# Second attention: a pair's scores in single PSUM banks, read by two VectorE instructions per head

## The chip, the cores and the metric

The kernel runs on one core of one Trainium2 chip. The metric is the device time of one execution in microseconds, the median over several runs. Times in stages and of single instructions come from one profiled execution. PE is TensorE's matmul, PEld its weight load, DVE VectorE, ACT ScalarE, POOL GpSimd, SP the engine whose queue issues the DMAs.

## The reference

A trunk of two layers over 1024 latent tokens and 256 context tokens of width 1024, in float32. Layer 0 mixes tokens by neighbourhood attention (16 heads of 64), layer 1 by sliding-window attention, and each ends with a gated feed-forward part with a short convolution. The change is in layer 1's attention: 16 query heads in 4 groups, each group with one key head and one value head. A block of 128 queries sees its own 128 keys, the 128 before and the 128 after, cut to a distance of 128, and all 256 context keys; a logit per head (the sink) enters the softmax without a value.

```python
def sliding_window_attention(q, k, v, k_c, v_c, sink):
    band = np.abs(qoff[:, None] - koff[None, :]) <= SWA_RADIUS
    ctx_ok = jnp.ones((Q_BLOCK, n_ctx), bool)
    def block_step(j):
        ...
        valid = band & ((kpos >= 0) & (kpos < seq))[None, :]
        mask = jnp.concatenate([valid, ctx_ok], axis=-1)
        return attend(q_j, jnp.concatenate([k_j, k_c], axis=1), jnp.concatenate([v_j, v_c], axis=1),
                      mask=mask, sink=sink)
```

`attend` scales the products by 1/8, adds the mask, takes the softmax over keys and sink in float32 and multiplies by the values.

## The kernel before

The program is one long recording of operations on five engines. Each big stage (first attention, its feed-forward part, second attention, its feed-forward part) has a planner, the class `Sched`: operations are entered with an engine (or two to choose from), an estimated duration, what they read and write, a priority `key`, and the buffers that they take (`acq`) and give back (`rel`). `run` then plays the stage through with these estimates and writes the instructions out in the order that comes out. On the chip each engine works through its instructions in that order and waits on semaphores where data or buffers are not ready. So the estimates set the order, and the chip sets the times.

The second attention goes over 4 groups (`g`). For each group, ten token tiles of 128 are projected to 4 query heads, a key and a value (matmuls into `mm`; then `qraw`, the norm by `qsq`, `qv`, `qy`, the rotary step by `qn`, `qa`, `qb`, and the split of queries and keys into two parts of lower precision, `st` and `klt`, which PE transposes into `q`, `kkl1`, `kll1` for latents and `kkc`, `klc` for context). Meanwhile the blocks of the group before are attended: 8 query blocks `j`, and in each two pairs of heads (`pr`), so 64 pairs, 128 heads. A pair is planned by `plan_su`, in these steps:

1. PE: scores of a head, queries times high and low part of the 256 context keys and of the block's 256 or 384 latent keys.
2. DVE: one pass that adds the mask and negates, min with the sink and down the row, to `S` in SBUF and the negated maximum in `m0` (shown as `m`). The instruction is `CUSTOM_DVE_ANT_0` in profiles and `ISA` in the orders below, and a short one behind it reads out its accumulator.
3. ACT: exponential of `S` in place, with the sum of the row into `sm`.
4. DVE: reciprocal of the sum; DVE or ACT: scaling of `S`.
5. PE: transposes of `S` into `pt`, DVE or ACT: copies out, PE: products with the values into `pv`.

In the kernel before, step 1 writes to `wide`, a PSUM tile of 1536 columns, which is three banks of 512. The columns are chosen so that a head's context and latents lie side by side and can be read by one instruction of 512 or 640 columns, with no matmul across a bank's border. In a middle block head 0 has its latents in columns 128 to 511 and its context in 512 to 767, head 1 its context in 768 to 1023 and its latents in 1024 to 1407. In step 4 both heads of a pair share one reciprocal instruction. The mask `bandt` has 1024 columns, zeros for the context among them, in two arrangements. The planner holds the two heads' places as two single buffers, `s0` and `s1`.

PSUM has eight banks: three for scores, and by tag `pt` 2, `mm` 2, `pv` 1. The first attention takes its scores from the tag `s` (three buffers of one bank), by the branch of `plan_su` without `wide`.

Of the kernel before, what the change touches and what calls it, by code (L numbers as in the profile page):

```python
# [11 lines left out]
F32 = mybir.dt.float32  # L12
# [229 lines left out]
def trunk_kernel(ctx, tc, xperm, xseq, cc, wmod, bmod, gnorm, na_wqkv, na_gq, na_gk, na_bias, na_wo,  # L242
# [184 lines left out]
    def t_pe(n):  # L427
        return max(0.107, 0.0125 + n / 2400.0)
# [170 lines left out]
    def plan_su(sc, key, I, units, groups, psa, wk, reads, wide=None, at=None):  # L599
# [22 lines left out]
        def qk(k):  # L622
            nl = units[k]["nl"]

            def f(e):
                u = J["u", k] = units[k]["get"]()
# [4 lines left out]
            return f  # L631

        if wide is not None:
            for k in range(2):
                nl = units[k]["nl"]
                sc.op("pe", 2 * t_pe(256) + 2 * t_pe(nl), qk(k), reads=reads, writes=[K("s", k)], key=key,
                      acq=[(f"s{k}", K("s", k), 1)], rel=units[k]["rel_c"] + units[k]["rel_l"])

                def scores(e, k=k, nl=nl):
                    if k == 0:  # L640
                        J["sm"] = tiny.tile([P, 2, 2], F32, tag="sm", name="sm", bufs=4)
                    n = TC + nl
                    o = min(at[k])
                    J["S", k] = SP["pool"].tile([P, SP["n"]], F32, tag="S", name="S", bufs=SBUFS)
                    J["m", k] = tiny.tile([P, 2], F32, tag="m0", name="m0", bufs=8)
                    dve.tensor_tensor_reduce(out=J["S", k][:, :n], in0=wide[:, o:o + n], in1=J["u", k]["mask"], scale=-1.0,
                                             scalar=J["u", k]["sink"], op0=ALU.add, op1=ALU.min, accum_out=J["m", k][:, 1:2])
                sc.op("dve", 0.29 + 0.00103 * (TC + nl), scores, reads=[K("s", k)], writes=[K("Sc", k)], key=key,
                      acq=[("S", K("S", k), uses[k])], rel=[K("s", k)])
        else:  # L650
            sc.op("pe", 4 * t_pe(256), qkc, reads=reads, writes=[K("sc")], key=key, acq=[("s", K("sc"), 2)],
                  rel=units[0]["rel_c"] + units[1]["rel_c"])
        for k in range(2):
            if units[k]["nl"] and wide is None:
# [39 lines left out]
        for k in range(2):  # L694
            n = TC + units[k]["nl"]

            def rec(e, k=k):
                if wide is None:
                    dve.reciprocal(J["sm"][:, k, 1:2], J["sm"][:, k, 0:1])
                else:  # L700
                    dve.reciprocal(J["sm"][:, :, 1], J["sm"][:, :, 0])
            if wide is None:
# [1372 lines left out]
    def tables():  # L2075
        fin = C1["pool"]
        for nm, shape in (("gqk", [P, 2, DH]), ("bandt", [P, 8 * P]), ("rc", [P, 8, 2, DH]),
                          ("rs", [P, 8, 2, DH])):
            C1[nm] = fin.tile(shape, F32, name=nm)
        C1["sink"] = small[:, 8:8 + H]  # L2080
# [92 lines left out]
    wide = ps.tile([P, 1536], F32, name="wide")  # L2173
# [4 lines left out]
    sc = Sched(dict(CAPS, pt2=3, q=7, s0=1, s1=1))  # L2178
# [3 lines left out]
    def plan_sw_qkv(n):  # L2182
# [105 lines left out]
        if lat:  # L2288
# [7 lines left out]
            def qev(e):  # L2296
                q = f["q"][tt] = fin.tile([P, 4, P], F32R, tag="q", name="q", bufs=7)
                copy(e, q.rearrange("p a b -> p (a b)"), J["pt"].bitcast(F32))
# [4 lines left out]
    def plan_sw_su(n):  # L2303
# [8 lines left out]
        for k in range(2):  # L2312
# [3 lines left out]
            m0 = P * (1 if j == 0 else 3 if j == 7 else (0, 3)[k])  # L2316

            def get(hd=hd, m0=m0, nl=nl):
                q = f["q"][j]
                return dict(q=q[:, hd, :], kk=kkl1[:, ks], kl=kll1[:, ks], kkc=f["kkc"], klc=f["klc"],  # L2320
                            mask=bandt[:, m0:m0 + TC + nl], sink=sink[:, 4 * g + hd:4 * g + hd + 1])
# [4 lines left out]
        nl = (hi - lo + 1) * P  # L2326

        at = ([(256, 512), (768, 1024)] if j == 0 else [(512, 256), (1024, 768)] if j == 7 else [(128, 512), (1024, 768)])
        c0 = [min(a) for a in at]
        lst = [(8 + i, *[at[k][1] - c0[k] + i * P for k in range(2)]) for i in range(2)]  # L2330
        lst += [(b, *[at[k][0] - c0[k] + (b - lo) * P for k in range(2)]) for b in range(lo, hi + 1)]
        lst = [(lambda t=t: f["v"][t], ("v", g, t), [(0, a), (1, b)]) for t, a, b in lst]
        f["half", pr] = plan_su(sc, key, I, units, [lst[i:i + 2] for i in range(0, len(lst), 2)], psa, wk, reads, wide, at)
# [121 lines left out]
def layout(i):  # L2455
# [36 lines left out]
    before, after, zero = band[:, :P], band[:, 2 * P:], np.zeros((P, P), np.float32)  # L2492
    a["band"] = np.concatenate([before, zero, after, zero, zero, before, zero, after], axis=1)
# [31 lines left out]
```

## Time and profile before

| what | value |
|---|---|
| median of 3 runs | 2887.53 us (2882.95 to 2894.57) |
| profiled execution, own time | 2894.24 us |
| its span, from first to last instruction | 2892.4 us |
| first attention, a stretch in the middle | 300 to 600 us |
| second attention | about 1725 to 2150 us |
| score matmuls into `wide` | 512, from 1725.3 to 2146.4 us |

Stretches are counted in us from the start of the span. A busy engine need not work at its full rate: matmuls overlap, and the profile gives each its whole length. The granted clock is TensorE's, 1.00 at full speed. A wait is put down to the instruction whose end released it.

### The profile page before, as it was taken

The page shows a single profiled execution, that of the slowest core. Times are in us where ns is not written, and L with a number is a line of the kernel's source. Part 1 is how long each engine was busy: PE and PEld are TensorE (multiplying, and loading weights), DVE is VectorE, ACT ScalarE, POOL GpSimd, SP SyncE. Part 2 cuts the span into 40 slices and gives each one's busy share as a digit, 9 for nine tenths or more (in the row PEclk, how much of TensorE's full clock was granted, in tenths as well). Part 3 has the DMA queues.
Part 4 walks back from the last instruction along what each step waited for, and adds up shares of the span by engine and source line. Part 5 has one row for each costly group of instructions (what it writes and reads, how often), then busy time and mean ns, then how long its engine had stood idle before and what let it go on. Part 6 is the DMA issues. An engine that isn't in the chain of part 4 may idle for free.

```text
span 2892.4 us, 44674 instructions
## 1 busy us (share of the span) xinstructions
PE 2800.7 (97%) x16344; PEld 2376.4 (82%) x16344; DVE 2155.3 (75%) x4581; ACT 1713.4 (59%) x3203; POOL 365.9 (13%) x572
## 2 busy tenths in 40 slices
PE   6999999999999999999999999999999899999999
PEld 4889898898799977777788887888878688888887
DVE  7767666678678677777786887666666888888767
ACT  4766666667456555555564557766773566656443
POOL 2111111112000000000000034534430000000000
PEclk8999999999999999999999999999999999999999
DMA  6222322224645544444475631000044332234655
GB/s 243 63 88 80 91 63 73 88 65 155 223 163 185 178 161 136 150 139 156 154 255 175 202 120 34 14 28 14 30 147 145 112 109 93 102 109 142 233 174 187
DMA packets 140365, 367.44 MB, mean 127 GB/s; under 512 B 20848, under 2 KB 33520, under 8 KB 138736
## 3 DMA queue, kind: packets, MB, share of 16 engines
q1 hardware_dynamic: 140144, 364.57, 38.2%
q8 instruction: 129, 2.11, 0.3%
q14 instruction: 92, 0.75, 0.1%
HBM read 297.53 MB, written 66.98 MB: 126 GB/s over the span
## 4 chain that ended last, share of the span: by engine, by line
PE 63%; DVE 8%; issue 2%; ACT 1%; POOL 1%; DMA 1%; POOLq 0%; DVEq 0%; SPq 0%; ACTq 0%
PE ua L79 17%; PE uc L79 13%; PE dn L79 12%; PE mm L79 5%; PE ud L79 4%; PE oacc L79 3%; PE wide L79 3%; DVE S L79 2%; PE pt L79 2%; PE dnc L79 2%; PE pv L79 2%; PE mod L79 1%; DVE wlo L79 1%; DVE xn L79 1%; DVE x L79 0%
## 5 line engine op out<-in xcount | busy, mean ns | idle before, releaser
L79 ACT ACTIVATE whi<-wraw 128x512 fp32r<-128x512 f32 (+1 forms) x264 | 211.9, 803 | 162.5 <-PE uc L79 52.8
L79 DVE TENSOR_TENSOR wlo<-wraw,whi 128x512 fp32r<-128x512 f32 (+1 forms) x264 | 240.4, 911 | 61.1 <-ACT whi L79 60.6
L79 ACT ACTIVATE S<-S,m 128x640 f32<-128x640 f32 (+3 forms) x288 | 220.4, 767 | 59.7 <-DVE m L79 43.3
L79 PE MATMUL dn<-ghi,whi 128*128 128x512 f32 x616 | 240.0, 390 | 0.0
L79 PE MATMUL dn<-glo,whi 128*128 128x512 f32 x616 | 239.8, 389 | 0.2 <-DVE glo L79 0.2
L79 PE MATMUL dn<-ghi,wlo 128*128 128x512 f32 x616 | 239.7, 389 | 0.0
L79 ACT ACTIVATE whi<-s 128x1024 fp32r<-128x1024 f32 (+1 forms) x120 | 113.2, 943 | 182.2 <-PE uc L79 124.1
L79 PE MATMUL pt<-idr,S 128*128 128x128 f32 x1280 | 191.0, 279 | 4.0 <-ACT pt L79 1.3
L79 ACT ACTIVATE ghi<-graw 128x512 fp32r<-128x512 f32 x154 | 96.0, 629 | 152.6 <-PE dn L79 94.6
L79 POOL TENSOR_TENSOR qy<-qv,mhalf 128x4 f32<-128x4 f32 (+2 forms) x120 | 126.1, 1051 | 469.1 <-DVE qv L79 457.9
L79 PE MATMUL mm<-whi,h0hi 128*128 128x384 f32 x512 | 181.7, 355 | 1.4 <-ACT qraw L79 1.4
L79 PE MATMUL mm<-wlo,h0hi 128*128 128x384 f32 x512 | 172.1, 336 | 0.0
L79 ACT ACTIVATE pt<-pt 128x512 f32<-128x512 f32 (+2 forms) x272 | 139.8, 531 | 52.3 <-PE pt L79 50.6
L79 PEld LDWEIGHTS pt<-idr,S 128*128 128x128 f32 x1280 | 150.5, 142 | 24.2 <-issue 5.9
L79 DVE TENSOR_TENSOR glo<-graw,ghi 128x512 fp32r<-128x512 f32 x154 | 106.2, 699 | 78.4 <-ACT ghi L79 45.9
L79 PE MATMUL pv<-pt,v 128*64 128x256 f32 (+1 forms) x1376 | 154.9, 370 | 0.3 <-DVE pt L79 0.3
L79 DVE TENSOR_TENSOR wlo<-s,whi 128x1024 fp32r<-128x1024 f32 (+1 forms) x120 | 129.6, 1080 | 25.6 <-ACT whi L79 25.3
L79 DVE CUSTOM_DVE_ANT_0 S<-wide,bandt,small 128x640 f32<-128x640 f32 (+1 forms) x128 | 107.7, 846 | 49.6 <-PE wide L79 46.7
L79 PE MATMUL ua<-t12hi,whi 128*128 128x512 f32 x352 | 138.9, 395 | 4.3 <-ACT t12hi L79 3.5
L79 PE MATMUL uc<-t34h,whi 128*128 128x512 f32 x352 | 140.1, 398 | 0.0
L79 DVE TENSOR_SCALAR_CACHE_REDUCE S<-s 128x256 f32<-128x256 f32 x160 | 64.4, 419 | 100.4 <-PE s L79 100.2
L79 PE MATMUL ua<-t12lo,whi 128*128 128x512 f32 x352 | 138.3, 393 | 0.9 <-DVE t12lo L79 0.9
(329 smaller groups left out, 8616.5 us busy)
## 6 DMA issues: line engine op xcount, KB each, us to landing
wraw<-in_w_up_dram SPq DMA_DIRECT2D x132, 512.0 KB, 3.3
wm<-in_wmod_dram SPq DMA_DIRECT2D x80, 512.0 KB, 4.1
wraw<-in_w_down_dram SPq DMA_DIRECT2D x44, 512.0 KB, 3.4
graw<-g_dram SPq DMA_DIRECT2D x44, 512.0 KB, 4.2
wraw<-in_w_down_dram SPq DMA_DIRECT2D x88, 256.0 KB, 3.1
graw<-g_dram SPq DMA_DIRECT2D x66, 256.0 KB, 2.8
slab<-in_na_wqkv_dram SPq DMA_DIRECT2D x32, 384.0 KB, 3.2
woraw<-in_na_wo_dram SPq DMA_DIRECT2D x24, 512.0 KB, 4.6
```

Source lines behind the costliest of these rows:

```text
L79: r = f(*a, **k)
```

## The change

In the second attention `wide` goes, and `plan_su` takes the branch that the first attention uses. The context scores of both heads of a pair go to one bank (256 columns each), the latent scores of each head to a bank of its own, all three from the tag `s`. DVE reads a head in two instructions: the context (a `TENSOR_SCALAR` that negates and takes the minimum with the sink; in profiles `TENSOR_SCALAR_CACHE_REDUCE`), and the latents with the mask, starting from the first one's maximum. Each head has a reciprocal of its own. The mask has 384 columns, and with the space there are 8 buffers of `q` in place of 7. The planner's estimates for these operations are those of the first attention.

```diff
-    def plan_su(sc, key, I, units, groups, psa, wk, reads, wide=None, at=None):
+    def plan_su(sc, key, I, units, groups, psa, wk, reads):
...
-                for o, a, b in ((at[k][1], "kkc", "klc"), (at[k][0], "kk", "kl")):
-                    n = TC if a == "kkc" else nl
-                    pe.matmul(wide[:, o:o + n], u["q"], u[a], start=True, stop=False, skip_group_check=True)
-                    pe.matmul(wide[:, o:o + n], u["q"], u[b], start=False, stop=True, skip_group_check=True)
...
-                    dve.tensor_tensor_reduce(out=J["S", k][:, :n], in0=wide[:, o:o + n], in1=J["u", k]["mask"], scale=-1.0,
-                                             scalar=J["u", k]["sink"], op0=ALU.add, op1=ALU.min, accum_out=J["m", k][:, 1:2])
-                sc.op("dve", 0.29 + 0.00103 * (TC + nl), scores, reads=[K("s", k)], writes=[K("Sc", k)], key=key,
-                      acq=[("S", K("S", k), uses[k])], rel=[K("s", k)])
-        else:
-            sc.op("pe", 4 * t_pe(256), qkc, reads=reads, writes=[K("sc")], key=key, acq=[("s", K("sc"), 2)],
-                  rel=units[0]["rel_c"] + units[1]["rel_c"])
+        sc.op("pe", 4 * t_pe(256), qkc, reads=reads, writes=[K("sc")], key=key, acq=[("s", K("sc"), 2)],
+              rel=units[0]["rel_c"] + units[1]["rel_c"])
...
-            if wide is None:
-                sc.op("dve", t_dve(TC) + 0.06, ctx_part, reads=[K("sc")], writes=[K("Sc", k)], key=key,
-                      acq=[("S", K("S", k), uses[k])], rel=[K("sc")])
+            sc.op("dve", t_dve(TC) + 0.06, ctx_part, reads=[K("sc")], writes=[K("Sc", k)], key=key,
+                  acq=[("S", K("S", k), uses[k])], rel=[K("sc")])
             parts = [K("Sc", k)]
-            if nl and wide is None:
+            if nl:
                 def lat_part(e, k=k, nl=nl):
...
-                    dve.reciprocal(J["sm"][:, :, 1], J["sm"][:, :, 0])
-            if wide is None:
-                sc.op("dve", 0.08, rec, reads=[K("P", k)], writes=[K("r", k)], key=key)
-            elif k == 0:
-                sc.op("dve", 0.09, rec, reads=[K("P", 0), K("P", 1)], writes=[K("r", 0), K("r", 1)], key=key)
+                dve.reciprocal(J["sm"][:, k, 1:2], J["sm"][:, k, 0:1])
+            sc.op("dve", 0.08, rec, reads=[K("P", k)], writes=[K("r", k)], key=key)
...
-    wide = ps.tile([P, 1536], F32, name="wide")
...
-    sc = Sched(dict(CAPS, pt2=3, q=7, s0=1, s1=1))
+    sc = Sched(dict(CAPS, pt2=3))
...
-        at = ([(256, 512), (768, 1024)] if j == 0 else [(512, 256), (1024, 768)] if j == 7 else [(128, 512), (1024, 768)])
...
-    a["band"] = np.concatenate([before, zero, after, zero, zero, before, zero, after], axis=1)
+    a["band"] = band
```

The order on PE changes from the first pair on. At the 32nd and 33rd pair (the last block of the second group and the first of the third, 1934 to 1939 us in the profile before; 256 latent keys in both blocks) PE had, with the semaphore that a row waits for in brackets:

```order
L79 MATMUL wide<-kll_18599,q 128x256
L79 MATMUL pt<-idr,st 128x128 [waits PE_49,Pool_49]
L79 MATMUL pt<-idr,st 128x128 x3
L79 MATMUL wide<-kkc,q 128x256 [waits DVE_49]
L79 MATMUL wide<-klc,q 128x256
L79 MATMUL wide<-kkl_18598,q 128x256
L79 MATMUL wide<-kll_18599,q 128x256
L79 MATMUL mm<-whi,h1hi_18097 128x384
L79 MATMUL mm<-whi,h1lo_18098 128x384
L79 MATMUL mm<-wlo,h1hi_18097 128x384
L79 MATMUL wide<-kkc,q 128x256 [waits DVE_49]
L79 MATMUL wide<-klc,q 128x256
```

and now has:

```order
L79 MATMUL s<-klc,q 128x256
L79 MATMUL s<-kkl_18597,q 128x256
L79 MATMUL s<-kll_18598,q 128x256
L79 MATMUL s<-kkl_18597,q 128x256
L79 MATMUL s<-kll_18598,q 128x256
L79 MATMUL mm<-whi,h1hi_18097 128x384
L79 MATMUL mm<-whi,h1lo_18098 128x384
L79 MATMUL mm<-wlo,h1hi_18097 128x384
L79 MATMUL mm<-whi,h1hi_18097 128x384
L79 MATMUL mm<-whi,h1lo_18098 128x384
L79 MATMUL mm<-wlo,h1hi_18097 128x384
L79 MATMUL s<-kkc,q 128x256 [waits DVE_49]
```

A pair's eight score matmuls stand together, and six projection matmuls stand between them and the next pair; before, each head's four waited for DVE's read of the head ahead of it.

On DVE, at the same two pairs, stood:

```order
L79 ISA S,m_21742<-wide,bandt,small 128x512 [waits PE_49]
L79 ISA m_21742 128x1
L79 TENSOR_REDUCE qv<-qsq 128x5 [waits Activation_49]
L79 ISA S,m_21763<-wide,bandt,small 128x512 [waits PE_49]
L79 ISA m_21763 128x1
L79 TENSOR_SCALAR qv<-qv 128x5 [waits DVE_49]
L79 ISA S,m_21775<-wide,bandt,small 128x512 [waits PE_49]
L79 ISA m_21775 128x1
L79 ISA S,m_21790<-wide,bandt,small 128x512 [waits PE_49]
L79 ISA m_21790 128x1
L79 TENSOR_TENSOR qt<-qy 128x5 [waits Pool_49]
L79 RECIPROCAL sm<-sm 128x2 [waits Activation_49]
```

and stands now:

```order
L79 TENSOR_SCALAR S,m_21935<-s,small 128x256 [waits PE_49]
L79 TENSOR_SCALAR S,m_21947<-s,small 128x256
L79 TENSOR_REDUCE qv<-qsq 128x5 [waits Activation_49]
L79 ISA S,m_21935<-s,bandt,m_21935 128x256 [waits DVE_49,PE_49]
L79 ISA m_21935 128x1
L79 TENSOR_SCALAR qv<-qv 128x5 [waits DVE_49]
L79 ISA S,m_21947<-s,bandt,m_21947 128x256 [waits PE_49]
L79 ISA m_21947 128x1
L79 TENSOR_SCALAR S,m_21976<-s,small 128x256 [waits PE_49]
L79 TENSOR_SCALAR S,m_21980<-s,small 128x256
L79 RECIPROCAL sm<-sm 128x1 [waits Activation_49]
L79 ISA S,m_21976<-s,bandt,m_21976 128x256 [waits DVE_49,PE_49]
```

The first rows are the two context reads of a pair from one bank, then a latent read for each head, which also waits for DVE's own earlier maximum; the reciprocal now serves one head.

Over the whole program the orders differ in these counts. PE has the same matmuls. DVE has 256 score reads in place of 128 in the second attention and 128 reciprocals in place of 64; of the scalings of `S` it has 211 in place of 176, and ACT 45 in place of 80. DVE makes 13 fewer copies out of `pt`, 14 fewer of `osb`, 10 more of `v`.

More of the change, by code (lines that the diff above doesn't have):

```diff
@@ L620, in qkl @@
             return f
[L622 to L626, printed above, removed]
-                for o, a, b in ((at[k][1], "kkc", "klc"), (at[k][0], "kk", "kl")):
-                    n = TC if a == "kkc" else nl
-                    pe.matmul(wide[:, o:o + n], u["q"], u[a], start=True, stop=False, skip_group_check=True)
-                    pe.matmul(wide[:, o:o + n], u["q"], u[b], start=False, stop=True, skip_group_check=True)
[L631 to L645, printed above, removed]
-                    dve.tensor_tensor_reduce(out=J["S", k][:, :n], in0=wide[:, o:o + n], in1=J["u", k]["mask"], scale=-1.0,
-                                             scalar=J["u", k]["sink"], op0=ALU.add, op1=ALU.min, accum_out=J["m", k][:, 1:2])
-                sc.op("dve", 0.29 + 0.00103 * (TC + nl), scores, reads=[K("s", k)], writes=[K("Sc", k)], key=key,
-                      acq=[("S", K("S", k), uses[k])], rel=[K("s", k)])
-        else:
-            sc.op("pe", 4 * t_pe(256), qkc, reads=reads, writes=[K("sc")], key=key, acq=[("s", K("sc"), 2)],
-                  rel=units[0]["rel_c"] + units[1]["rel_c"])
+        sc.op("pe", 4 * t_pe(256), qkc, reads=reads, writes=[K("sc")], key=key, acq=[("s", K("sc"), 2)],
+              rel=units[0]["rel_c"] + units[1]["rel_c"])
         for k in range(2):
-            if units[k]["nl"] and wide is None:
+            if units[k]["nl"]:
                 sc.op("pe", 2 * t_pe(units[k]["nl"]), qkl(k), reads=reads + [K("sc")], writes=[K("sl", k)], key=key,
@@ L2076, in tables @@
         fin = C1["pool"]
-        for nm, shape in (("gqk", [P, 2, DH]), ("bandt", [P, 8 * P]), ("rc", [P, 8, 2, DH]),
+        for nm, shape in (("gqk", [P, 2, DH]), ("bandt", [P, 3 * P]), ("rc", [P, 8, 2, DH]),
                           ("rs", [P, 8, 2, DH])):
@@ L2320, in get @@
                 return dict(q=q[:, hd, :], kk=kkl1[:, ks], kl=kll1[:, ks], kkc=f["kkc"], klc=f["klc"],
-                            mask=bandt[:, m0:m0 + TC + nl], sink=sink[:, 4 * g + hd:4 * g + hd + 1])
+                            mask=bandt[:, m0:m0 + nl], sink=sink[:, 4 * g + hd:4 * g + hd + 1])
             units.append(dict(nl=(hi - lo + 1) * P, sink=1, get=get, mask_key=[], rel_c=[("q", g, j), ("kkc", g), ("klc", g)],
@@ L2325, in plan_sw_su @@
         reads += [(x, t) for t in range(lo, hi + 1) for x in ("kk", "kl")]
-        nl = (hi - lo + 1) * P
-        at = ([(256, 512), (768, 1024)] if j == 0 else [(512, 256), (1024, 768)] if j == 7 else [(128, 512), (1024, 768)])
-        c0 = [min(a) for a in at]
-        lst = [(8 + i, *[at[k][1] - c0[k] + i * P for k in range(2)]) for i in range(2)]
-        lst += [(b, *[at[k][0] - c0[k] + (b - lo) * P for k in range(2)]) for b in range(lo, hi + 1)]
+        lst = [(8 + i, i * P, i * P) for i in range(2)] + [(b, *[TC + (b - lo) * P] * 2) for b in range(lo, hi + 1)]
         lst = [(lambda t=t: f["v"][t], ("v", g, t), [(0, a), (1, b)]) for t, a, b in lst]
-        f["half", pr] = plan_su(sc, key, I, units, [lst[i:i + 2] for i in range(0, len(lst), 2)], psa, wk, reads, wide, at)
+        f["half", pr] = plan_su(sc, key, I, units, [lst[i:i + 2] for i in range(0, len(lst), 2)], psa, wk, reads)
         if pr == 0:
@@ L2491, in layout @@
     band = np.where(np.abs(q - k) <= 128, 0.0, NEG).astype(np.float32)
-    before, after, zero = band[:, :P], band[:, 2 * P:], np.zeros((P, P), np.float32)
-    a["band"] = np.concatenate([before, zero, after, zero, zero, before, zero, after], axis=1)
+    a["band"] = band
     a["w_up"] = np.stack([_lay_w(i["ffn_w_up"][l]) for l in range(2)])
```

7 lines of the change are left out of this document (2 added, 5 removed).

## The prediction

> **What bounds the kernel now.** I read the page first, then the stretches of the second attention against those of the first, then who waited for whom in it, then its chain of waits, and last single instructions. The first row below is the page's; the others are stretches (start and end in us, length, busy us with instructions of PE, PEld, DVE, ACT and POOL, then the granted clock, the DMA share and GB/s).
>
> ```profile
> PE 2800.7 (97%) x16344; PEld 2376.4 (82%) x16344; DVE 2155.3 (75%) x4581; ACT 1713.4 (59%) x3203; POOL 365.9 (13%) x572
> ...
> 300.00:600.00 300.00, 299.62 (x2205) 267.98 (x2203) 211.02 (x830) 198.91 (x506) 54.52 (x62) 1.00 0.28 82
> 1725.00:2150.00 425.00, 392.92 (x2701) 334.01 (x2701) 286.36 (x781) 310.60 (x734) 198.43 (x385) 0.96 0.12 38
> 1725.00:1760.00 35.00, 32.04 (x230) 27.69 (x229) 28.02 (x74) 29.19 (x71) 23.37 (x49) 1.00 0.03 9
> ```
>
> PE is busy 97% over the span, but not evenly. In the stretch 300 to 600, which is the first attention, it idles 0.4 us in 300. The second attention fills 1725 to 2150: 425 us, PE idle for 32, and a clock of 0.96. Everything that the change touches runs here, about 15% of the span, so the answer is read from this stage. DVE is busy 286/425 = 67% of it, ACT 73%; in its first 35 us DVE is at 28/35 = 80%.
>
> Who PE and DVE wait for in that stage (us in total, times, longest):
>
> ```profile
> PE wide L79 <- DVE m L79: 23.5, 41, 1.9
> PE pt L79 <- DVE pt L79: 3.6, 2, 2.2
> ...
> DVE S L79 <- PE wide L79: 46.7, 59, 2.6
> DVE v L79 <- ACT qraw L79: 26.0, 15, 4.2
> DVE pt L79 <- PE pt L79: 19.6, 18, 2.4
> DVE sm L79 <- ACT S L79: 14.4, 16, 1.6
> ```
>
> Of PE's 32 idle us, 23.5 are one wait: score matmuls into `wide` held until DVE has finished reading it. The timeline shows how (the first two rows are PE, the next three DVE, the last PE; in brackets the idle time and its releaser):
>
> ```profile
> 1934.28 0.28 PE L79 MATMUL wide<-kll,q 128*128 128x256 f32 x1
> 1934.40 0.45 PE L79 MATMUL pt<-idr,st 128*128 128x128 f32 x4
> ...
> 1934.61 0.75 DVE L79 CUSTOM_DVE_ANT_0 S<-wide,bandt,small 128x512 f32<-128x512 f32 x1 [1.45 <-PE wide L79]
> 1935.28 0.08 DVE L79 DVE_READ_ACCUMULATOR2_ANT m<- 128x1 f32 x1
> 1935.28 0.48 DVE L79 TENSOR_REDUCE qv<-qsq 128x5 f32<-128x320 f32 x1
> ...
> 1935.42 0.39 PE L79 MATMUL wide<-kkc,q 128*128 128x256 f32 x1 [0.57 <-DVE m L79]
> ```
>
> Head 0 of the pair is written by 1934.5, DVE reads it from 1934.61 to 1935.36, and only then does PE write head 1, although its columns are others. The two heads share the middle bank (head 0 has its context in columns 512 to 767, head 1 in 768 to 1023), so they take turns. The chain of waits of the stage, and of its first 35 us, by line:
>
> ```profile
> by line: PE mm L79 22.2%; PE wide L79 18.4%; DVE S L79 14.0%; PE pt L79 12.9%; PE pv L79 11.9%; POOL qb L79 2.0%; POOL qy L79 1.9%; issue 1.7%; DVE v L79 1.6%; DVE qv L79 1.4%; POOL qa L79 1.3%; DVE klt L79 1.3%; DVE qt L79 1.3%; ACT S L79
> ...
> by line: PE wide L79 20.3%; DVE S L79 18.4%; PE mm L79 12.2%; PE pv L79 12.1%; PE pt L79 11.3%; DVE qt L79 7.9%; ACT S L79 6.4%; POOL qy L79 3.3%; DVE v L79 2.6%; DVE qa L79 2.1%; issue 1.9%; DVE klt L79 1.4%; ACT qraw L79 1.4%; ACT st L79
> ```
>
> DVE carries 14.0 + 1.6 + 1.4 + 1.3 + 1.3 = 19.6% of the chain, or 29% of the time that it is busy (19.6/67). In the first 35 us, where it is 80% busy, it carries 18.4 + 7.9 + 2.6 + 2.1 + 1.4 = 32.4%, or 40% of its busy time: the fuller DVE is, the more of its work counts.
>
> **The change, part by part.** Durations (mean ns after the comma) are from these groups, the first eight from the second attention and the last three from the first, where scores already come as context and latents apart:
>
> ```profile
> L79 DVE CUSTOM_DVE_ANT_0 S<-wide,bandt,small 128x640 f32<-128x640 f32 x96 | 83.9, 879 | 37.4 <-PE wide L79 34.7 <-PE pt L79 1.9 <-POOL o0lo L79 0.6
> L79 DVE TENSOR_SCALAR S<-S,sm 128x640 f32<-128x640 f32 x51 | 30.3, 603 | 0.5
> L79 DVE COPY pt<-pt 128x512 f32<-128x512 f32 x37 | 25.2, 685 | 12.3 <-PE pt L79 12.2
> L79 DVE CUSTOM_DVE_ANT_0 S<-wide,bandt,small 128x512 f32<-128x512 f32 x32 | 23.8, 747 | 12.2 <-PE wide L79 12.0
> ...
> L79 DVE RECIPROCAL sm<-sm 128x2 f32<-128x2 f32 x64 | 10.2, 160 | 16.3 <-ACT S L79 16.1
> L79 DVE COPY v<-qraw 128x64 f32<-128x64 f32 x21 | 9.8, 468 | 26.2 <-ACT qraw L79 26.0
> ...
> L79 DVE COPY osb<-pv 128x256 f32<-128x256 f32 x18 | 7.5, 419 | 1.1 <-PE pv L79 1.1
> ...
> L79 DVE TENSOR_SCALAR S<-S,sm 128x512 f32<-128x512 f32 x13 | 6.7, 518 | 0.1
> ...
> L79 DVE TENSOR_SCALAR_CACHE_REDUCE S<-s 128x256 f32<-128x256 f32 x74 | 29.9, 419 | 57.4 <-PE s L79 57.4
> L79 DVE CUSTOM_DVE_ANT_0 S<-s,bias,m 128x384 f32<-128x384 f32 x43 | 26.0, 611 | 0.8
> ...
> L79 DVE CUSTOM_DVE_ANT_0 S<-s,bias,m 128x256 f32<-128x256 f32 x16 | 7.7, 482 | 0.6
> ```
>
> *Score matmuls.* Their number and sizes stay; only their order and banks change. PE's own work: 0.
>
> *Bank waits.* Counting the matmuls between two uses of one bank, at the start-to-start distances of the timeline, 72 of 127 reuses of the middle bank have under 1 us of PE work between them before, none of 141 after; 28 have 1 to 2.5 us. DVE must fit two context reads or one latent read in between, 0.84 or 0.61 us plus the way there and back. I let those 28 wait 0.33 us each, as the smaller waits now do: 9 us of the 23.5 stay. Gain 14.5 us. Bounds: 23.5 (none stays) and 7.5 (28 waits at the mean of today's, 23.5/41 = 0.57 us).
>
> *Two DVE reads per head for one.* 128 x 0.419 + 96 x 0.611 + 32 x 0.482 = 127.7 us for 83.9 + 23.8 = 107.7: 20.0 us more.
>
> The Trainium skill speaks against this part: "VectorE: DVE Perf Modes", in its rules for kernel authors, says to minimise the count of operations, and its table of costs gives a PSUM read a fixed 120 cycles. By it the split would cost about 128 x 0.125 = 16 us (an estimate from that page) for my 20.0, and the sum would come out a microsecond or two lower; the trace's own rows decide here.
>
> *A reciprocal per head.* 128 for 64 at 0.160: 10.2 us.
>
> *Work that the planner moves along with it.* By the two orders DVE gets 35 scalings from ACT (32 x 0.603 + 3 x 0.518 = 20.9 us), 10 copies of `v` (4.7) and some ten small tensor products (about 5), and gives ACT 13 evacuations of transposes (8.6) and 14 of `osb` (5.9): 16 us more. ACT loses about as much, at 73% busy and with hardly a place on the chain: 0.
>
> DVE's sum is 20 + 10 + 16 = 46 us by durations. Its instructions overlap, though: in the rows above the read of the accumulator and the reduction start at 1935.28, 0.67 us into a 0.75 us instruction. At 0.07 us for each of some 220 instructions more, 15 come off: 31 us, and DVE would be (286 + 31)/425 = 75% busy. What of it lands on the chain? Bounds: nothing, as in the first attention, where DVE is 211/300 = 70% busy and PE idles 0.4 us; or all 31. I take the 40% of the fullest stretch, since the load comes near it: 12.5 us.
>
> *The smaller mask and the eighth `q` buffer.* The mask is one load, about 200 us ahead of its use (it is issued during the feed-forward layer before, with DMA engines half idle), and no wait on `q` stands among PE's: 0 both; if the cover were gone, it would be the load's 6.9 us:
>
> ```profile
> bandt<-in_band_dram SPq DMA_DIRECT2D x1, 512.0 KB, 6.9
> ```
>
> Sum: -14.5 + 12.5 = -2. Against the profiled execution's own 2894.2 us that is **2892 us**. That execution stands at the top of the three runs shown and 6.7 us above their median, 2887.5, so by the median my figure reads "no change, within 0.5%" (14.4 us, about what a measurement of this kernel can tell).
>
> **The rivals.**
>
> *DVE becomes the bound: slower.* DVE is in order, and its idle time is mostly spent waiting at the head of its queue (46.7, 26.0, 19.6, 14.4 us above), not spare. A context read that waits for PE then holds the previous pair's scalings behind it, and these hold the transposes. For it: two score reads of a pair become four, the stage is fuller than the first attention on POOL (198/425 against 55/300), and a head's second read now waits for its own first one. Price: all 31 us on the chain, bank waits down by 7.5: +23.5, or 2918. It decides above (14.5 + 7.7)/31 = 72% of DVE's extra work on the chain. Against it: the first attention lives with the same pattern.
>
> *The cover holds: faster.* All 23.5 us of bank waits go, DVE's extra stays hidden, and the clock comes back. These two stretches show the clock:
>
> ```profile
> 1878.00:1884.00 6.00, 3.79 (x28) 3.21 (x26) 6.00 (x9) 2.08 (x8) 4.68 (x6) 0.93 0.52 151
> 1884.00:1892.00 8.00, 7.58 (x31) 7.42 (x31) 4.19 (x14) 3.71 (x7) 4.81 (x10) 0.50 0.25 81
> ```
>
> PE idles 2.2 of 6 us, then works 8 us at half clock. Over the stage a clock of 0.96 is 17 us lost; half of it back is 8.5. Price: -23.5 - 8.5 = -32, or 2862. The Trainium skill has the mechanism in "TensorE: Matmul & The Clock Gate", under what is actually happening: the gate halves the clock after an idle window of 3.4 us and opens after a busy one. By that rule the 8.5 would come back only if the long gaps at the start of each group close; the trace agrees in that the half clock follows such a gap. Against this rival: the gap at 1878 has DVE busy all 6 us, so it is DVE work, not a bank, that makes it.
>
> *The wait only moves* (to the transposes, whose scalings now come one head at a time): the sum then is near 0, inside my own case.
>
> **How the numbers follow.** The trade (bank waits for DVE work) gets 0.39, with its own range 2880 to 2904; DVE as the bound 0.36; the cover 0.25. Two of the cases lie on opposite sides, so the range must reach both: 2862 to 2920. The first case lies within 0.5% of the median, the second above, the third below, which gives 0.25 faster, 0.39 same, 0.36 slower.
>
> **What would show it.** In the changed profile, in the stage from 1725 on: score matmuls waiting for DVE at about 9 us in place of 23.5; DVE near 317 busy us; two score groups of some 54 and 74 us; 128 reciprocals; ACT's scalings down by 35; PE's matmul counts the same. If DVE's idle time shrinks to under a sixth of the stage and PE waits at `pt` for scaled `S`, the second case holds. If PE idles under 10 us and the clock reads 0.99, the third does. The forecast is wrong if the time lies outside 2880 to 2904; the step to blame first is the 40%, which is taken from a single stretch.

## The result: 36 us faster, where no change was forecast

| | before | after |
|---|---|---|
| median of 4 runs each | 2888.26 us (2882.95 to 2894.57) | 2852.33 us (2851.94 to 2853.17) |
| ratio, with its 95% interval | 1 | 0.9875 (0.9855 to 0.9895) |
| profiled execution, own time and span | 2894.24 and 2892.4 us | 2852.58 and 2850.8 us |
| last score matmul of the second attention starts at | 2146.4 us | 2106.1 us |

The gain is 2888.26 - 2852.33 = 36 us, and outside the forecast's range. First the stretches of the profile after, in the columns used in the prediction (start and end in us, length, busy us with instructions of PE, PEld, DVE, ACT and POOL, granted clock, DMA share, GB/s): the second attention, all that follows it, and the first 35 us of the second attention.

```profile
1725.00:2110.00 385.00, 375.23 (x2694) 322.06 (x2694) 305.46 (x1125) 295.17 (x714) 189.25 (x366) 0.99 0.13 42
2110.00:2850.00 740.00, 728.13 (x3252) 593.28 (x3250) 568.89 (x753) 386.92 (x522) 2.76 (x3) 0.99 0.41 142
1725.00:1760.00 35.00, 33.85 (x245) 28.13 (x246) 32.43 (x118) 31.95 (x79) 23.82 (x45) 1.00 0.06 18
```

The same 2700 matmuls now take 385 us in place of 425, and the part behind the stage takes 740 us, where it took 742: nearly everything came from the stage. PE idles 385 - 375.2 = 9.8 us there in place of 32.1, which is 22 us. PE's busy time fell from 392.9 to 375.2, by 18 us, and the granted clock (the third number from the right, 0.50 or 1.00 in these rows) tells where most of that comes from. First the stretches at half clock of the stage before, then the whole stage after, but for its edges:

```profile
1763.70:1767.00 3.30, 3.30 (x14) 2.67 (x16) 2.04 (x6) 2.67 (x5) 2.99 (x7) 0.50 0.28 105
1883.20:1893.30 10.10, 9.56 (x43) 9.21 (x42) 4.99 (x17) 4.50 (x9) 5.71 (x10) 0.50 0.27 77
1995.80:2006.00 10.20, 9.62 (x42) 9.27 (x42) 5.09 (x18) 4.41 (x9) 5.72 (x10) 0.50 0.01 3
2108.40:2118.60 10.20, 7.37 (x26) 6.16 (x27) 5.13 (x15) 6.00 (x12) 4.12 (x9) 0.50 0.43 161
...
1725.00:2070.00 345.00, 336.81 (x2444) 292.72 (x2444) 267.27 (x1005) 261.66 (x639) 172.00 (x337) 1.00 0.09 31
2070.10:2076.80 6.70, 5.65 (x19) 4.35 (x19) 6.20 (x19) 4.87 (x11) 4.44 (x10) 0.50 0.72 262
2077.00:2110.00 33.00, 32.47 (x233) 24.70 (x231) 31.69 (x103) 28.34 (x66) 12.71 (x20) 1.00 0.35 112
```

PE ran at half clock for 34 us of the stage before, which loses 17, and for 7 us of it after, which loses 3.4: another 13.6. About 4 of the 40 are left. A score matmul right behind a wait is longer, 0.39 us in the prediction's row where the three behind it take 0.28; with 41 such waits before and 6 after this makes 35 x 0.1 = 3.5 us, an estimate.

Who PE waits for in the stage after the change, and who DVE waits for (us in total, times, longest):

```profile
PE pt L79 <- DVE klt L79: 2.2, 3, 0.9
PE s L79 <- DVE m L79: 2.1, 5, 0.9
PE pt L79 <- DVE S L79: 1.0, 1, 1.0
...
PE s L79 <- DVE S L79: 0.4, 1, 0.4
...
DVE S L79 <- PE s L79: 26.8, 18, 5.2
DVE pt L79 <- PE pt L79: 12.8, 6, 3.5
DVE klt L79 <- ACT st L79: 11.4, 9, 2.2
```

Score matmuls wait for DVE for 2.1 + 0.4 = 2.5 us in place of 23.5. DVE's own work from 1705 to 2130 us, by groups (busy us, mean ns, idle time before):

```profile
L79 DVE TENSOR_SCALAR_CACHE_REDUCE S<-s,small 128x256 f32<-128x256 f32 x128 | 59.5, 476 | 24.2 <-PE s L79 23.8
L79 DVE CUSTOM_DVE_ANT_0 S<-s,bandt,m 128x384 f32<-128x384 f32 x96 | 58.3, 611 | 5.4 <-PE s L79 3.0 <-PE pt L79 0.5
L79 DVE TENSOR_SCALAR S<-S,sm 128x640 f32<-128x640 f32 x83 | 49.5, 596 | 1.1
L79 DVE RECIPROCAL sm<-sm 128x1 f32<-128x1 f32 x128 | 20.0, 158 | 9.4 <-ACT S L79 8.4
...
L79 DVE CUSTOM_DVE_ANT_0 S<-s,bandt,m 128x256 f32<-128x256 f32 x32 | 15.1, 476 | 0.6
...
L79 DVE TENSOR_SCALAR S<-S,sm 128x512 f32<-128x512 f32 x16 | 7.8, 489 | 0.3
```

DVE does what the diff says: two reads a head, 128 reciprocals, 99 scalings. It is busy 305 of 385 us, 79%. The chain of waits of the stage (shares by line) shows what this costs:

```profile
by line: PE mm L79 18.0%; PE pt L79 14.7%; DVE S L79 13.0%; PE pv L79 10.8%; PE s L79 9.1%; issue 7.9%; ACT S L79 5.7%; POOL qy L79 2.5%; POOL qb L79 2.0%; POOL qa L79 1.8%; DVE qa L79 1.5%; DVE qv L79 1.3%; ACT st L79 1.2%; DVE qn L79 1.2%
```

PE's scores fell from 18.4% to 9.1%. DVE, with more work in a shorter stage, carries 13.0 + 1.5 + 1.3 + 1.2 = 17.0% of the chain in the lines that the row names, where it carried 19.6%.

### The profile page after: what moved, and what is told of

It reads as the page before. It is cut to its first block, busy times and chain, and to the rows that moved or that the text cites. A ratio compares the mean times of both kernels' runs of the same rounds, so it can differ in the third digit from the quotient of the medians.

```text
span 2850.8 us, 45105 instructions
## 1 busy us (share of the span) xinstructions
PE 2784.9 (98%) x16344; PEld 2367.3 (83%) x16344; DVE 2176.6 (76%) x4931; ACT 1699.5 (60%) x3185; POOL 361.3 (13%) x560
## 4 chain that ended last, share of the span: by engine, by line
PE 63%; DVE 6%; issue 3%; ACT 2%; POOL 1%; DMA 1%; POOLq 0%; DVEq 0%; SPq 0%; ACTq 0%
PE ua L79 17%; PE dn L79 14%; PE uc L79 13%; PE mm L79 4%; PE ud L79 4%; PE oacc L79 3%; PE pt L79 2%; DVE S L79 2%; PE dnc L79 2%; PE pv L79 2%; PE s L79 1%; PE mod L79 1%; ACT S L79 1%; DVE x L79 0%; DVE wlo L79 0%
## 5 line engine op out<-in xcount | busy, mean ns | idle before, releaser
L79 ACT ACTIVATE pt<-pt 128x512 f32<-128x512 f32 (+2 forms) x285 | 146.4, 533 | 40.1 <-PE pt L79 37.3
L79 PE MATMUL ua<-t12hi,wlo 128*128 128x512 f32 x352 | 137.7, 391 | 0.0
```

What stands on the lines that cost most here:

```text
L79: r = f(*a, **k)
```

## Experiments

The trace tells that the turns of the two heads at the middle bank are gone. It does not tell what took them away: the new layout, the split reads, or the order in which the instructions now stand. The theory, A where an expectation gives it a letter: the planner was the cause. With `s0` and `s1` it held the two heads' places for independent, so it set head 1's matmuls right behind head 0's, and on the chip PE then waited for DVE's read of head 0. Any form of the scores whose turns the planner knows should then be as fast, fused read or not. Rivals: the layout itself; the estimate of the fused read; the shared reciprocal; and DVE's load, which could be near to deciding.

All results, each against runs of the kernel before beside it (a row of dashes separates what was run together). Differences below are between medians; the kernel before had 2888.26, 2890.89, 2890.34, 2888.88 and 2889.41 us as its median beside the kernel after and in the four sets, so a difference of 2 or 3 us across sets says nothing.

| kernel | median, us (lowest to highest) | ratio to before (95%) |
|---|---|---|
| own_banks_fused_mm1 | 2879.68 (2875.82 to 2881.41) | 0.9962 (0.9948 to 0.9976) |
| after_mm1 | 2887.45 (2883.08 to 2889.04) | 0.9988 (0.9978 to 0.9997) |
| after_by_head | 2869.72 (2867.84 to 2872.48) | 0.9930 (0.9915 to 0.9945) |
| before_turns_known | 2852.98 (2852.22 to 2853.80) | 0.9871 (0.9857 to 0.9886) |
| --- | | |
| before_prefetch_held | 2893.86 (2883.56 to 2896.63) | 1.0010 (0.9999 to 1.0021) |
| before_read_estimate | 2889.41 (2884.55 to 2891.95) | 0.9999 (0.9989 to 1.0009) |
| after_context_read_twice | 2909.00 (2907.39 to 2909.86) | 1.0065 (1.0050 to 1.0080) |
| after_one_reciprocal | 2866.08 (2862.33 to 2867.92) | 0.9916 (0.9901 to 0.9930) |
| --- | | |
| turns_known_two_reciprocals | 2850.12 (2848.36 to 2854.33) | 0.9859 (0.9840 to 0.9878) |
| turns_known_two_reciprocals_estimate | 2858.59 (2855.62 to 2862.25) | 0.9887 (0.9867 to 0.9908) |
| after_context_read_twice_planned | 2869.42 (2869.24 to 2871.74) | 0.9926 (0.9908 to 0.9944) |
| before_two_reciprocals | 2886.76 (2883.29 to 2891.54) | 0.9990 (0.9979 to 1.0001) |
| --- | | |
| after_by_head_known | 2867.60 (2864.13 to 2870.26) | 0.9920 (0.9899 to 0.9942) |
| after_prefetch_held | 2853.18 (2851.98 to 2855.98) | 0.9872 (0.9848 to 0.9896) |

### The planner is told of the turns, and nothing else: before_turns_known

```diff
-                      acq=[(f"s{k}", K("s", k), 1)], rel=units[k]["rel_c"] + units[k]["rel_l"])
+                      acq=[("s0", K("s", k), 1)], rel=units[k]["rel_c"] + units[k]["rel_l"])
...
-            op1.weights(dt, sw_wo[dt % KT], OKEY + dt, KT)
+            op1.weights(dt, sw_wo[dt % KT], OKEY + dt, KT, [("oraw", 0, kt) for kt in range(6)] if dt == 4 else [])
```

Both heads now take one buffer of the plan, so head 1's matmuls are planned behind DVE's read of head 0. Tile, banks, fused read and shared reciprocal stay. The second line only makes the prefetch of one piece of output weights start later; the plan needs it to reach the end of the stage.

> The kernel before, except that both heads claim one place in the planner, so that it knows that they take turns and puts other work between; the same prefetch is held back. Theory A in its form that the planner's ignorance is the cost: bank waits fall under 10 us and the time comes down by 10 to 25 us, to 2863 to 2878. If the turns themselves cost, whoever knows of them: no gain, 2880 to 2895. Theory B: no gain either.

Measured: 2852.98, the whole gain of the change (ratio 0.9871 against 0.9875, the intervals almost the same), and more than the 10 to 25 us that its own theory had expected. It is no single lucky order: the three kernels with fused reads whose plan knows the turns have medians of 2850 to 2859 us, and the four whose plan does not (the kernel before and three variants of it) 2887 to 2894. Its timeline some 20 us ahead of the place where the prediction showed the turns, again with two heads of 256 latent keys (rows of PE and DVE; start, duration):

```profile
1914.13 0.28 PE L79 MATMUL wide<-kkc,q 128*128 128x256 f32 x1
...
1914.49 0.29 PE L79 MATMUL wide<-kll,q 128*128 128x256 f32 x1
1914.62 0.34 PE L79 MATMUL mm<-whi,h1hi 128*128 128x384 f32 x1
...
1915.34 0.74 DVE L79 CUSTOM_DVE_ANT_0 S<-wide,bandt,small 128x512 f32<-128x512 f32 x1
...
1916.01 0.07 DVE L79 DVE_READ_ACCUMULATOR2_ANT m<- 128x1 f32 x1
...
1916.55 0.33 PE L79 MATMUL mm<-wlo,h1hi 128*128 128x384 f32 x1
1916.73 0.28 PE L79 MATMUL wide<-kkc,q 128*128 128x256 f32 x1
```

Between the scores of the one head and those of the next stand twelve projection matmuls, 2.1 us of work. DVE's read ends at 1916.08, while they run, 0.65 us before the place is wanted again. The turns are still taken; PE has other work meanwhile. By the distances in the two traces, 1 to 6 of the 127 reuses have under 1 us of PE work between them, where 63 to 76 had (the lower counts use the distances as they are, the upper the median for each kind of matmul; the prediction counted 72). In the trace the wait is down to these (us, times, longest):

```profile
PE wide L79 <- DVE m L79: 6.6, 4, 3.9
```

### The later prefetch alone: before_prefetch_held, after_prefetch_held

> The kernel before with the one prefetch of output weights held back as in before_turns_known and after_by_head, and nothing else. If the planner's knowledge of the turns gave the 38 us of before_turns_known, this stays within 6 us of the kernel before (2885 to 2897). If the prefetch did it, it comes near 2853.

> The changed kernel with the prefetch held back, nothing else: within 4 us of 2852 if the hold is as neutral here as in before_prefetch_held; if it is not, the 17 us of after_by_head and of after_context_read_twice_planned are smaller by what it costs.

Only the second line of the diff above, in either kernel. Before stays at 1.0010 (0.9999 to 1.0021), with the same 23.4 us of waits for the bank, and after at 2853.18 against its 2852.33. The line is no part of the gain.

### The layout without the split read: own_banks_fused_mm1 and after_mm1

```diff
-    wide = ps.tile([P, 1536], F32, name="wide")
+    wide = [ps.tile([P, 1024], F32, name=f"wide{k}") for k in range(2)]
...
-        at = ([(256, 512), (768, 1024)] if j == 0 else [(512, 256), (1024, 768)] if j == 7 else [(128, 512), (1024, 768)])
+        at = [(256, 512) if j == 0 else (512, 256)] * 2
...
-    sc = Sched(dict(CAPS, pt2=3, q=7, s0=1, s1=1))
+    sc = Sched(dict(CAPS, mm=1, pt2=3, q=7, s0=1, s1=1))
```

Each head has two banks of its own, read by one fused instruction, so that there are no turns. That takes four banks for scores, and the projections keep one (`mm=1`). The kernel after with one bank for projections is its partner.

> The kernel before with its one DVE read per head, but each head has two banks to itself (four banks for scores), so no bank is shared; the bank for it is taken from mm, which has one buffer in place of two. Read against the next run, the changed kernel with one mm buffer. Theory A (the shared bank made the two heads take turns, and this was the loss): waits of score matmuls for DVE in the second attention fall from 23.5 us to under 6, and the time is within 8 us of the next run's. Theory B (the single read itself, its place in DVE's queue or its too long estimate in the planner, was the loss): it stays 20 us or more above the next run.

> The changed kernel with one mm buffer in the second attention, the other half of the pair. One buffer costs a wait per projected tile: about 40 tiles at 0.5 us, so 2852 + 5 to 20 us by either theory.

Measured: the lost bank costs the kernel after 2887.45 - 2852.33 = 35 us, more than expected, so that the pair says little of the full kernels. Between the partners the fused read is the faster one, by 2887.45 - 2879.68 = 8 us, and PE's wait for a bank of scores is 3.5 us:

```profile
PE wide L79 <- DVE m L79: 3.5, 4, 1.5
```

So the fused read is not the trouble. In this pair it costs nothing where the heads' banks are apart.

What the two heads share was not separated further: here each has a tile as well as banks of its own. In the kernel before, the wait does not hang on the middle bank alone. In the first block of the second, third and fourth groups, head 1's context goes to columns 1024 to 1279, the third bank, and head 0's read covers columns 256 to 767, the first two; yet the first matmul of head 1 waits for that read:

```profile
1937.79 0.75 DVE L79 CUSTOM_DVE_ANT_0 S<-wide,bandt,small 128x512 f32<-128x512 f32 x1 [0.75 <-PE wide L79]
1938.47 0.08 DVE L79 DVE_READ_ACCUMULATOR2_ANT m<- 128x1 f32 x1
...
1938.61 0.39 PE L79 MATMUL wide<-kkc,q 128*128 128x256 f32 x1 [0.33 <-DVE m L79]
```

So the program's wait may be for the tile `wide` as a whole. For the argument this makes no difference: the turns are there, and the plan did not know them.

### The split read with heads one by one: after_by_head, after_by_head_known

```diff
-        sc.op("pe", 4 * t_pe(256), qkc, reads=reads, writes=[K("sc")], key=key, acq=[("s", K("sc"), 2)],
-              rel=units[0]["rel_c"] + units[1]["rel_c"])
+        for k in range(2):
+            sc.op("pe", 2 * t_pe(256) + 2 * t_pe(units[k]["nl"]), qk(k), reads=reads, writes=[K("sc", k), K("sl", k)], key=key,
+                  acq=([("s", K("sc"), 2)] if k == 0 else []) + [("s", K("sl", k), 1)], rel=units[k]["rel_c"] + units[k]["rel_l"])
```

A head's context and latents are written by one step of the plan, into the banks of the kernel after: the context's bank is shared as before, and the plan does not know that head 1's half has to wait for the read of head 0's. The second kernel adds this to its `reads` (`reads + ([K("Sc", 0)] if k else [])`) and enters head 1's step behind head 0's reads. Both have the later prefetch. (In the files this stands under a flag that only the second attention sets; `qk`, which writes a head's four matmuls, is not shown.)

> The changed kernel with its two DVE reads and its banks, but PE writes the scores head by head (context and latents of head 0, then of head 1), so that the shared context bank is taken in turns again and the planner does not know it. One prefetch of output weights in the stage's tail is held back a little. Theory A: bank waits come back, 12 to 25 us of score matmuls waiting for DVE, and most of the gain goes: 2870 to 2890 us. Theory B: the reads stay as they are in the changed kernel, so it stays within 6 us of 2852.

> after_by_head with one thing more: the planner places head 1's score matmuls behind DVE's context read of head 0, as the shared context bank has it on the chip. If turns that the plan does not know were what cost after_by_head its 17 us: 2850 to 2860. If writing by head costs by itself (latents later, DVE's queue longer): 2865 to 2875.

Measured: 17 us of the gain go (2869.72 against 2852.33), but telling the planner brings back hardly any (2867.60, the intervals overlap): here theory A's expectation failed. So did the expected 12 to 25 us of bank waits: PE waits for score banks only 4.8 us in the first of them, although its time falls just short of the expected 2870 to 2890. Its loss is elsewhere, as its chain of waits shows:

```profile
by line: DVE S L79 28.5%; PE mm L79 12.1%; PE pt L79 9.0%; PE s L79 6.9%; PE pv L79 5.4%; issue 5.3%; DVE qa L79 4.6%; DVE qn L79 3.1%; DVE pt L79 3.1%; DVE klt L79 2.7%; DVE qt L79 2.2%; POOL qa L79 1.9%; POOL qb L79 1.8%; DVE sm L79 1.7%;
```

DVE carries 28.5 + 4.6 + 3.1 + 3.1 + 2.7 + 2.2 + 1.7 = 46% of the chain, where the kernel after has 17%. The second one, as slow, has another chain:

```profile
by line: PE mm L79 16.5%; DVE S L79 15.9%; PE pt L79 13.4%; PE s L79 8.7%; PE pv L79 7.8%; issue 5.9%; ACT S L79 4.9%; DVE qa L79 3.6%; POOL qy L79 2.6%; DVE qv L79 2.3%; DVE qt L79 2.3%; DVE qn L79 2.1%; DVE pt L79 1.6%; DVE klt L79 1.5%; 
```

There DVE carries 29%, so its share of the chain does not tell the price either. With split reads, writing the context of both heads at once is worth some 15 us; what costs them without it was not settled. Knowing the turns is thus not enough in every layout, and not knowing them cost hardly anything in this one.

### The read's estimate: before_read_estimate, turns_known_two_reciprocals_estimate

```diff
-                sc.op("dve", 0.29 + 0.00103 * (TC + nl), scores, reads=[K("s", k)], writes=[K("Sc", k)], key=key,
+                sc.op("dve", 0.14 + 0.00103 * (TC + nl), scores, reads=[K("s", k)], writes=[K("Sc", k)], key=key,
```

> The kernel before with the planner's estimate of the single read brought down to the chip's start-to-start time (0.14 us + 0.00103 us per column in place of 0.29, so 0.80 for 640 columns); the places stay as they were, so the turns stay unknown. Theory A (unknown turns): no gain, 2882 to 2898. Theory B (a wrong estimate set the order badly): 2855 to 2875.

> The run before with the planner's estimate of the read at 0.14 in place of 0.29 us + 0.00103 us per column. Now that the plan holds, the estimate could tell: 3 to 8 us faster than the run before if a plan with true times is better, slower by as much if the spare 0.15 us per read is what keeps PE from meeting DVE late.

The estimate gave 0.82 us for the read of 512 columns, which the trace shows at 0.747. In the kernel before, a smaller one changes nothing (0.9999), and the bank's waits are 29.5 us:

```profile
PE wide L79 <- DVE m L79: 29.5, 39, 2.4
```

Where the planner knows the turns, the smaller one loses 2858.59 - 2850.12 = 8 us (the two sets of runs do not touch, though the intervals of their ratios do). The estimate is no cause of what before lost, and with the turns known the generous figure is the better one.

### The reciprocal: after_one_reciprocal, before_two_reciprocals, turns_known_two_reciprocals

```diff
-                dve.reciprocal(J["sm"][:, k, 1:2], J["sm"][:, k, 0:1])
-            sc.op("dve", 0.08, rec, reads=[K("P", k)], writes=[K("r", k)], key=key)
+                dve.reciprocal(J["sm"][:, :, 1], J["sm"][:, :, 0])
+            if k == 0:
+                sc.op("dve", 0.09, rec, reads=[K("P", 0), K("P", 1)], writes=[K("r", 0), K("r", 1)], key=key)
```

This is the edit of the first, for the second attention; the other two do the reverse, in the kernel before (with the later prefetch) and in before_turns_known.

> The changed kernel with one reciprocal instruction per pair in place of two, 64 DVE instructions of 0.16 us fewer, but a head's scaling waits for both exponentials. If DVE's extra work costs nothing: 2848 to 2858. If 40% of it counts: 4 us less, about 2848. If the coupling of the two heads was part of the loss before: 2860 to 2870.

> The kernel before with a reciprocal per head and the turns still unknown (prefetch held). If the heads are held together by the bank anyway, nothing is won: 2882 to 2897. If the shared reciprocal was a good part of the loss: 2870 to 2880.

> before_turns_known with a reciprocal per head, as in the changed kernel: the single read per head with the turns in the plan and the heads uncoupled. In the changed kernel the shared reciprocal costs 14 us; if that holds here too, 2835 to 2845, faster than the changed kernel and 31 us less DVE work than it. If the turns tie the heads together anyway: 2848 to 2858.

A reciprocal per head, which the prediction booked as 10.2 us more for DVE, is worth 2866.08 - 2852.33 = 14 us in the kernel after. In before_turns_known (3 us of medians, 0.9871 against 0.9859 with overlapping intervals) and in the kernel before (0.9990, 0.9979 to 1.0001) it is worth nothing that the runs tell apart. A shared one waits for the exponentials of both heads before either can be scaled; how much of the 14 us is this and how much another order was not separated.

turns_known_two_reciprocals keeps the fused reads, the shared bank, the wide mask and seven `q` buffers, and has known turns and two reciprocals. At 0.9859 (0.9840 to 0.9878) it is the fastest that ran, though not to be told from the kernel after at 0.9875 (0.9855 to 0.9895). So layout, 128 more reads, smaller mask, eighth `q` buffer and the later prefetch together make no difference that these runs can tell (2 us of medians, in favour of the fused reads).

### A suspected cost doubled: after_context_read_twice, and the same planned

```diff
-                dve.tensor_scalar(out=J["S", k][:, :TC], in0=J["sc"][:, k * 256:k * 256 + 256], scalar1=-1.0,
-                                  ...
+                for _ in range(2 if u["sink"] is not None else 1):
+                    dve.tensor_scalar(out=J["S", k][:, :TC], in0=J["sc"][:, k * 256:k * 256 + 256], scalar1=-1.0,
+                                      ...
```

DVE reads each context twice, 128 instructions more. The first kernel keeps the plan's estimate; the second doubles it (`(t_dve(TC) + 0.06) * 2`) and has the later prefetch.

> The changed kernel in which DVE reads each head's context scores twice in the second attention (same result, 128 more reads of 0.477 us, 61 us by duration, some 45 us start to start, which the planner does not know). This asks how much more DVE work the stage hides. By the 40% of the prediction: +18 us, 2870. If DVE still has cover at 78% busy: within 6 us of 2852. If the stage is at its edge: +30 us or more.

> The changed kernel with the context read twice, as in after_context_read_twice (2909 us), but with the planner told the doubled duration, and the prefetch held. If the added DVE work has no room whatever the plan: 2900 to 2912. If what costs is that the order is not made for it: 2860 to 2885.

Unplanned, they cost 2909.0 - 2852.3 = 57 us, of 128 x 0.480 = 61 that DVE is busy with them; planned, 2869.4 - 2852.3 = 17 us, 28%. The reads are the same. The chains of waits, first the unplanned kernel's:

```profile
by line: DVE S L79 41.6%; issue 10.7%; PE pt L79 5.0%; PE mm L79 4.8%; ACT S L79 4.2%; DVE qa L79 3.7%; DVE qv L79 3.0%; DVE pt L79 2.7%; DVE qn L79 2.6%; PE s L79 2.3%; POOL qy L79 2.3%; DVE sm L79 2.0%; POOL qb L79 1.8%; DVE qt L79 1.7%; 
```

and the planned one's:

```profile
by line: DVE S L79 30.8%; PE mm L79 14.3%; PE pt L79 11.5%; PE pv L79 7.6%; PE s L79 5.9%; issue 4.8%; ACT S L79 3.1%; DVE qa L79 3.1%; DVE pt L79 2.6%; DVE qn L79 2.3%; DVE qv L79 1.6%; DVE sm L79 1.4%; DVE qt L79 1.4%; DVE klt L79 1.3%; P
```

In both DVE has the largest part of the chain, but only in the second do PE's projections and transposes (14.3 and 11.5% in place of 4.8 and 5.0%) stand beside it. So work that the plan does not know can cost nearly its full length. That the orders of all engines, laid out without it, are the reason is theory A's reading; the pair of runs shows the price.

## Why the prediction was wrong, point by point

The prediction forecast no change; the kernel came out at 2852 us, below its 2880 to 2904 and below the wider 2862 to 2920. Two steps failed, by about as much: the 40% of DVE's extra work that was put on the chain (+12.5, nothing shown), and the clock, which the sum put at nothing (13.6 us came back). In the stage, against the profile before, bank waits gave 21, the clock 13.6, the shorter matmuls about 4, and PE's other idle time went from 32.1 - 23.5 = 8.6 us to 9.8 - 2.5 = 7.3: 40 in all.

*What bounds the kernel.* Right in the place (the second attention, PE held by the heads' turns) and not in the reason. The prediction took the shared bank for the fault. before_turns_known keeps the bank and has the whole gain: the fault was that the plan did not know of the turns. The evidence was at hand, in `s0` and `s1` as two single buffers for places in one tile. (The columns that the prediction names are those of a middle block; in the last block, which its timeline shows, the middle bank holds head 0's latents and head 1's context.)

*Bank waits, -14.5.* Mis-sized: 21 us went (23.5 to 2.5). The 28 reuses with 1 to 2.5 us of work between them were given 0.33 us each; five short waits for `m` and one for `S` are left.

*The clock, left out of the sum.* The likeliest case had no term for it; the one reason to be found stands with the third rival, that the gap before the half clock is DVE work, and it holds only by half (see the rivals). The clock gave 13.6 us: of 34 us at half clock 7 are left. The prediction's sentence on "TensorE: Matmul & The Clock Gate" of the Trainium skill, that the clock comes back only if the long gaps close, was borne out: of three long stretches at half clock two are gone, and PE idles 22 us less. The idle window of 3.4 us that it takes from that page is not what this trace shows: in the 5 us before each stretch at half clock of the stage before, PE's idle time adds up to 2.0 to 2.3 us, at the three long ones in pieces of 1.3 us at most.

*Two reads for one, +20.0; reciprocals, +10.2; moved work, +16.* The durations came out near: reads 59.5 + 58.3 + 15.1 = 132.9 us against 127.7 forecast, reciprocals 20.0 against 20.4, scalings 20.3 more against 20.9. The net load was overrated: DVE is 305 us busy, 19 more, not 31. Which of the moved work was less than booked was not followed up.

*40% of it on the chain, +12.5.* This step failed, and it is the one named to be blamed first. The share of DVE's busy time that lies on the chain of the fullest stretch is an average over work that is there, not the price of work that is added. In the same first 35 us DVE is now busy 32.43/35 = 93%, and PE idles 1.15 us, less than the 3.0 before. How much added work costs depended on the plan: of 61 us of reads 93% came through unplanned and 28% planned, of the change's own extra work nothing that the runs can tell (2850.12 with fused reads against 2852.33), and in the kernel after the reciprocals even paid. The Trainium skill's advice to minimise the count of operations ("VectorE: DVE Perf Modes", rules for kernel authors) was quoted against the change. The 128 reads more, for which the prediction's estimate from that page was some 16 us, took 25 us more of DVE's time (132.9 against 107.7), and of the kernel's, with layout, mask and buffer, no more than those 2 us.

*The mask and the eighth buffer, 0.* Right as far as shown: they are inside those 2 us.

*The rivals.* By the marks set down for it the cover held: PE idles under 10 us, and the clock reads 0.99. Its price, 2862, was 10 us short, chiefly because it gave back half of the clock's loss (8.5 us) and 13.6 came, and because it had no term for the 4 us of shorter matmuls. The argument set against it, that the gap at 1878 is DVE work and no bank, was half wrong: 1.1 of the 2.1 us there is a score matmul waiting for DVE's read of the head before.

```profile
1880.46 0.38 PE L79 MATMUL wide<-kkc,q 128*128 128x256 f32 x1 [1.12 <-DVE m L79]
```

By the marks of the second rival DVE is not the bound: it idles 21% of the stage, more than a sixth. As the bound it is real, but elsewhere: it has the largest part of the chain in after_by_head and with the doubled reads. That no more than 0.25 stood on the cover comes from the same wrong step, a full DVE read as a late one.

## What to carry to other kernels

Where a planner sets the order, ask first of a wait whether the plan knows it: a resource shared on the chip and separate in the plan can cost more than its own waits (36 us here for 23.5 of waits; the clock's loss came on top), and one tag can cure it. Not in every layout: after_by_head_known, told of its turns, won nothing that the runs tell apart. Price added work by whether it is planned, not only by how busy its engine is: the same 128 reads cost 17 us planned and 57 unplanned. Operations that are merged across heads save work on one engine and join two dependency chains; the merged reciprocal lost 14 us in the kernel after, for the 10 of DVE that it saved, and nothing that the runs tell apart in the two kernels with fused reads.

## What was not expected of the hardware

The context read of 256 columns takes 476 ns in the second attention, with the sink from SBUF as its second operand (`small`), where the same instruction without it takes 419 in the first. And the kernels differ in how well they repeat: the kernel before ran between 2882.95 and 2894.57 us in the first comparison, the kernel after between 2851.94 and 2853.17. Known turns alone do not do it, since turns_known_two_reciprocals ran between 2848.36 and 2854.33. What makes a kernel scatter was not tried.
